# Taking the conditioning's products two rows of blocks at a time

## The chip, the cores and the metric

The kernel runs on one core of a Trainium2 chip. The metric is device time in microseconds (us) of one launch. Engines are named as the profile names them: PE is TensorE's matmul, PEld its weight load, DVE VectorE, ACT ScalarE, POOL GpSimd, SP the engine that issues most of the loads. A "record" is one matmul as the trace shows it; the float32 products of the conditioning have two records each.

## The reference

Two blocks run one after the other over 512 tokens of 1024 channels. The first has two layers with a mixer (an mLSTM, a Fourier mixing and a convolution) and an MLP, over x and 256 further tokens of context; the second has attention and is not touched here. Each layer of the first block is conditioned: two vectors (`c` and `c_ctx`) are multiplied by a matrix of 1024 x 6144 a layer, and the six parts of 1024 shift, scale and gate the norms:

```python
for l in range(DEPTH):
    mx = jnp.split((jax.nn.silu(c) @ w_ada[l] + b_ada[l])[:, None, :], 6, axis=-1)
    mc = jnp.split((jax.nn.silu(c_ctx) @ w_ada[l] + b_ada[l])[None, None, :], 6, axis=-1)
    hx = modulate(rmsnorm(x, g_pre_mix[l]), mx[0], mx[1])
    hc = modulate(rmsnorm(ctx, g_pre_mix[l]), mc[0], mc[1])
    out_x, out_c = token_mixers(hx, hc, ...)
    x = x + mx[2] * rmsnorm(out_x, g_post_mix[l])
    hx = modulate(rmsnorm(x, g_pre_mlp[l]), mx[3], mx[4])
    x = x + mx[5] * rmsnorm(sq_relu_mlp(hx, w_mlp1[l], w_mlp2[l]), g_post_mlp[l])
```

So `w_ada` is 48 MB of weights for two vectors: much to load, little to multiply. Everything is float32.

## The kernel before, in words

The program is written once, in the order of the computation, through a `Recorder`; nothing is issued then. `schedule` orders each engine's instructions by priority and readiness with estimated durations, and gives each buffer its place, kind by kind, from a fixed number (`KINDS`: 3 raw weights `wr`, 2 high parts `wh`, 2 low parts `wl`, 4 and 3 PSUM banks `pm` and `pd`, 1 bank `pa`). Then everything is issued engine by engine in that order, and each engine runs its stream strictly in order, waiting for the others by semaphores. All recorded instructions stand on one line of the source (L358), so rows are told apart by their tiles.

A weight tile (`weight`) is a load of 512 KB into `wr`, a copy to `wh` by ACT (the high part), a subtraction to `wl` by DVE (the low part), and then three products a block on PE: high by high, high by low, low by high. In the MLP of the first block, `strassen` takes two weight tiles at once, forms sums of their quarters (on POOL and DVE, in place in `wr`) and makes seven products of quarters. Names: `wr<-in_w_in` are weights of the mixers, `wr<-in_w_mlp` of the MLP, `wr<-in_w_ada` rows of the conditioning.

The conditioning is cut into 12 units (`l`, `u`: two layers with six parts) of 8 rows of blocks each. `ada_steps` (L528 to 540) makes a list of 8 small functions for a unit. One such step loads a row, 128 x 1024, into a `wr` buffer and multiplies it: four products of 256 columns each (`128*32 128x256`, 32 stationary columns), which go to four sets of 32 rows of one PSUM tile `pa`. After the eighth row `ada_end` copies the sums from PSUM (`ftmp<-pa`, DVE), turns them on PE and adds the biases on DVE.

The steps are run from other code, to lie beside its work:

- the first two units at the start, from buffers of the kind `slot` (rows `pa<-slot,const`);
- 16 steps in the mixers of layer 0: `feed` holds them, and `weight` (L453) and `strassen` (L1301, twice a call) pop one step for each weight tile;
- 24 steps in the mLSTM outputs of layer 0 and 16 in those of layer 1 (list `back`, popped evenly over the chunks, L1172);
- 24 steps in the MLP of layer 0 (`feed.extend(mid)`, L1381), popped as the weight tiles come: 4 in `plain`, then in turn 4 in four weight tiles of `product2` and 2 in each of two calls of `strassen` (`fast`), and so on.

A run of products on `pa` between other work on PE is called a visit below. The program's text:

Of the kernel before, what the change touches and what calls it, by code (L numbers as in the profile page):

```python
# [33 lines left out]
# which engine takes the pairs of a norm's steps: v for Vector, p for Pool, a for Activation  # L34
ADD, MUL, AFF, LO = "vpvp", "vvvv", "avav", "vpvp"
# buffers: how many there are, and how many have to stay free when one is taken out of turn
# [8 lines left out]
class View:  # L45
    """A region of a buffer that gets its place only when the order of the instructions is known."""
# [49 lines left out]
    def bits(self):  # L96
        """the columns as the bits of a number"""
        m = np.zeros(self.buf.cols, np.uint8)
        m[self.idx.reshape(-1)] = 1
        return int.from_bytes(np.packbits(m).tobytes(), "big")  # L100
# [36 lines left out]
class Recorder:  # L137
    """Takes the program as it is written, orders each engine's instructions by priority and readiness with
    estimated durations, places the buffers, and then issues everything in that order."""
# [86 lines left out]
    def schedule(self):  # L226
        """List scheduling. A buffer's kind is served in program order."""
# [32 lines left out]
        def place(o):  # L260
            """places the buffers that the instruction is the first to touch, if they are all to be had"""
# [99 lines left out]
def tile_net(tc: tile.TileContext, A, out):  # L361
# [55 lines left out]
    def csum(srcs, n, w=0):  # L417
        """the mean over the channels of some blocks, on every partition"""
        ps = pm()[:, :n]
        for i, x in enumerate(srcs):  # L420
            pe.matmul(ps, onesD[:, w], x, start=i == 0, stop=i == len(srcs) - 1)
        return ps
# [7 lines left out]
    def add_square(acc, o, sl, n, first):  # L430
        """adds the squares of a block to a tile of sums"""
# [16 lines left out]
    feed = []  # L448
    HP, EP, RP = 3000, 3500, 100

    def weight(src, place=("wh", "wl"), nk=8, by=HP):
# [6 lines left out]
        if feed:  # L458
            feed.pop(0)()
# [23 lines left out]
    def run(blocks, acts, evac, order=R8, nk=None):  # L483
        """blocks: (key, source, groups); one weight tile after the other, all its tokens"""
# [5 lines left out]
    def narrow(src, acts, groups, evac):  # L490
        """a block of 32 columns: its high and low parts side by side, their products in two sets of rows"""
# [15 lines left out]
    def run_outer(blocks, acts, evac, groups, done=None, order=R8, ready=(), before=None):  # L507
        """as run, but group by group over a few resident weight tiles"""
# [19 lines left out]
    def ada_steps(l, u, place="wr"):  # L528
        st = K()

        def step(k):
            if k == 0:
                st.ps = pa()
            raw = rec.buf(place, [P, 1024], F32)
            ld(raw, A["w_ada"][l, u, k])
            for j in range(4):
                pe.matmul(st.ps[32 * j:32 * j + 32, 0:TC], cs[:, k, :], raw[:, j * TC:(j + 1) * TC], start=k == 0, stop=k == 7)
            if k == 7:
                ada_end(l, u, st.ps)
        return [lambda k=k: step(k) for k in range(8)]  # L540
# [23 lines left out]
    def pre(l, kind):  # L564
        """the gain and shift before the mixers (0) or the MLP (2), by conditioning"""
# [9 lines left out]
    def modulate(r, g, hs, gs, rs):  # L575
        """the next input of the matrix products: r * rs * gain + shift, in the two parts, r as four pairs of blocks"""
# [46 lines left out]
    def post_chain(g, o_, qs, old, hs, gs, gain=None):  # L623
        """the residual plus norm(o), kept in o's place and in DRAM, then the next norm"""
# [19 lines left out]
    def pairs():  # L644
        """activations in two parts: four tiles of [part, block of the pair, token]"""
# [26 lines left out]
    def rope_tables():  # L672
        """the cosines and signed sines by position, kept in DRAM until the second block"""
# [64 lines left out]
    def rows_of_three():  # L738
        """rows of the tokens of x, three to a slot"""
# [9 lines left out]
    class Later:  # L749
        """the tokens of x alone, by their place among all"""  # L750
# [7 lines left out]
    def gates(S, GX):  # L758
# [26 lines left out]
        # each head has two rows: the first of them takes the high part, the second the low one  # L785
# [46 lines left out]
    def mixers(l, hs, back, steps):  # L832
# [6 lines left out]
        # Fourier input and half of the conv module's  # L839
# [11 lines left out]
        # Fourier mixing: the sums over pairs of tokens s and n - s feed the cosines, the differences the sines,  # L851
        # and the results for t and n - t share both
# [46 lines left out]
        # conv module input  # L899
# [71 lines left out]
        # keys, values, queries  # L971
# [43 lines left out]
        # output gate  # L1015
# [10 lines left out]
        # mLSTM states before each chunk, both directions  # L1026
# [28 lines left out]
        # mLSTM outputs  # L1055
# [130 lines left out]
    # ---- the MLP's first product: tokens in two halves (A and B), channels in two halves, and the pairs of hidden  # L1186
    # blocks make seven products of quarters instead of eight (Strassen's algorithm as Winograd has it)
    def taker(n):
        """places for pairs of blocks of 256 tokens: first one in each of n slots, then their other two thirds, then more slots"""
# [81 lines left out]
    def strassen(l, src1, src2, parts_of, quarters, b, ev1, tail):  # L1271
# [14 lines left out]
        # the sums S2, S4 take the place of A11, A12 and S3, S1 that of A21, A22 when those have been split  # L1286
# [14 lines left out]
        for _ in range(2):  # L1301
            if feed:
                feed.pop(0)()
# [39 lines left out]
    def layer(l, hs, nxt, steps, back, mid, early=None, norm_mem=None, fill=None):  # L1343
# [7 lines left out]
        # output projection  # L1351
# [28 lines left out]
        # MLP  # L1380
# [189 lines left out]
    def block2(hs):  # L1570
# [8 lines left out]
        # selected and window keys and values, first queries: every block is chosen and the window covers the sequence  # L1579
# [505 lines left out]
```

## Time and profile before

| | us |
|---|---|
| runs | 2058.71, 2059.37, 2061.32 (median 2059.37) |
| span of the profiled execution | 2061.5 |
| PE busy | 1965.2 (95%) |
| PE weight loads busy | 1672.1 |
| DVE busy | 1386.3 |
| ACT busy | 878.3 |
| POOL busy | 501.9 |

The page gives the span of the profiled execution, from its first to its last instruction; it lies 0.1% above the median of the runs and within 0.2 us of the slowest. Busy shares are averages over stages with different limits; for a single stage the timeline and the stretches are read. A line of the timeline merges neighbouring instructions of one form: start, duration from the first's start to the last's end, and xcount. Neighbours on PE overlap, so that what a group costs the stream is the time from its start to the next line's start. Square brackets at a line's end are idle time before it and who ended it.

### The profile page before, as it was taken

How to read it: one execution, taken by the hardware profiler on the slowest of the kernel's cores; microseconds unless marked ns; L12 is line 12 of the kernel's file. 1: busy time of each engine (PE TensorE's matmuls, PEld its weight loads, DVE VectorE, ACT ScalarE, POOL GpSimd, SP SyncE). 2: the span in 40 equal slices, each digit the busy share in tenths (PEclk: the TensorE clock that was granted, in tenths of full speed). 3: DMA queues.
4: the chain of work that ended last, by engine and by line, in shares of the span. 5: the costliest groups of instructions: out<-in, count | busy, mean ns of one | idle time of the engine just before them, and what ended most of it. 6: DMA issues, size and time to landing. Idle time of an engine off the chain costs nothing.

```text
span 2061.5 us, 32412 instructions
## 1 busy us (share of the span) xinstructions
PE 1965.2 (95%) x12772; PEld 1672.1 (81%) x12772; DVE 1386.3 (67%) x2380; ACT 878.3 (43%) x1699; POOL 501.9 (24%) x486
## 2 busy tenths in 40 slices
PE   5999998988999999999899998899999998999999
PEld 3978885877988999999788886788989897776676
DVE  6588677287545665566878775887787785465664
ACT  4433355454322332234543355544343464553442
POOL 2210141245211222113320051542232232111210
PEclk8999998999999999999999999999999999999999
DMA  8233335251433221122321234322323342200201
GB/s 296 89 106 104 122 129 185 76 185 52 132 104 123 72 73 41 62 83 103 118 84 52 72 134 164 103 82 93 113 83 123 117 162 81 83 31 32 79 26 59
DMA packets 82570, 207.47 MB, mean 101 GB/s; under 512 B 8945, under 2 KB 36849, under 8 KB 82418
## 3 DMA queue, kind: packets, MB, share of 16 engines
q1 hardware_dynamic: 66690, 189.13, 27.0%
q10 hardware_dynamic: 15728, 16.27, 2.3%
q8 instruction: 100, 1.64, 0.3%
q14 instruction: 52, 0.43, 0.1%
HBM read 189.12 MB, written 16.25 MB: 100 GB/s over the span
## 4 chain that ended last, share of the span: by engine, by line
PE 65%; DVE 8%; issue 2%; ACT 1%; POOL 1%; DMA 1%; DVEq 0%; POOLq 0%; ACTq 0%
PE pd L358 44%; PE pm L358 18%; DVE slot L358 5%; PE pa L358 4%; DVE tmp L358 2%; DVE wl L358 1%; POOL slot L358 1%; ACT slot L358 0%; DMA wr<-in_w_ada 0%; ACT tmp L358 0%; ACT rs L358 0%; ACT wh L358 0%; DVE small L358 0%; POOL ftmp L358 0%; DMA wr<-in_w_in 0%
## 5 line engine op out<-in xcount | busy, mean ns | idle before, releaser
L358 PE MATMUL pd<-slot,wh 128*128 128x256 f32 (+2 forms) x4384 | 1092.2, 341 | 18.4 <-DVE slot L358 12.4
L358 PEld LDWEIGHTS pd<-slot,wh 128*128 128x128 f32 (+1 forms) x4384 | 745.1, 189 | 127.6 <-issue 18.7
L358 PE MATMUL pd<-slot,wl 128*128 128x256 f32 (+1 forms) x2136 | 724.1, 340 | 5.8 <-DVE wl L358 5.6
L358 PEld LDWEIGHTS pd<-slot,wl 128*128 128x128 f32 x2136 | 406.8, 191 | 55.0 <-DVE wl L358 7.7
L358 ACT ACTIVATE wh<-wr 128x1024 fp32r<-128x1024 f32 (+2 forms) x202 | 205.0, 1015 | 425.0 <-PE pd L358 388.1
L358 DVE TENSOR_TENSOR wl<-wr,wh 128x1024 fp32r<-128x1024 f32 (+2 forms) x199 | 248.4, 1248 | 129.1 <-ACT wh L358 128.2
L358 PE MATMUL pm<-slot,slot 128*128 128x256 f32 (+4 forms) x1674 | 256.7, 297 | 2.1 <-DVE tmp L358 1.6
L358 PEld LDWEIGHTS pm<-slot,slot 128*128 128x128 f32 (+1 forms) x1674 | 216.7, 191 | 28.2 <-issue 14.4
L358 DVE TENSOR_TENSOR slot<-pd,slot 128x512 f32<-128x512 f32 (+1 forms) x208 | 119.4, 574 | 127.0 <-PE pd L358 124.4
L358 PE MATMUL pd<-slot,slot 128*128 128x256 f32 (+1 forms) x1048 | 146.9, 289 | 2.9 <-ACT slot L358 2.6
L358 PEld LDWEIGHTS pd<-slot,slot 128*128 128x128 f32 x1048 | 132.8, 191 | 7.6 <-ACT slot L358 3.8
L358 DVE TENSOR_TENSOR slot<-ftmp,slot 128x512 fp32r<-128x512 f32 (+2 forms) x116 | 93.5, 809 | 36.1 <-POOL ftmp L358 34.5
L358 ACT ACTIVATE tmp<-tmp 128x512 f32<-128x512 f32 (+3 forms) x122 | 62.2, 545 | 126.9 <-DVE tmp L358 125.8
L358 DVE SCALAR_TENSOR_TENSOR slot<-slot,const,slot 128x512 f32<-128x512 f32 (+2 forms) x184 | 113.2, 664 | 0.8
L358 POOL TENSOR_TENSOR ftmp<-tmp 128x512 f32<-128x512 f32 x54 | 58.5, 1104 | 214.5 <-ACT tmp L358 214.5
L358 POOL TENSOR_TENSOR wr<-wr 128x512 f32<-128x512 f32 x27 | 39.3, 1455 | 290.0 <-DVE wl L358 248.9
L358 POOL TENSOR_TENSOR ftmp<-ftmp 128x256 f32<-128x256 f32 (+1 forms) x72 | 66.1, 918 | 166.7 <-ACT ftmp L358 162.5
L358 ACT ACTIVATE slot<-tmp 128x512 fp32r<-128x512 f32 (+1 forms) x134 | 80.7, 628 | 58.8 <-DVE tmp L358 38.8
L358 DVE TENSOR_TENSOR slot<-wr,slot 128x512 fp32r<-128x512 f32 (+1 forms) x85 | 87.3, 1033 | 17.2 <-ACT slot L358 17.2
L358 PE MATMUL pm<-slot,wh 128*128 128x256 f32 x544 | 98.4, 281 | 0.0
L358 ACT ACTIVATE slot<-wr 128x512 fp32r<-128x512 f32 (+1 forms) x85 | 72.0, 855 | 44.7 <-POOL wr L358 22.4
L358 PEld LDWEIGHTS pm<-slot,wh 128*128 128x128 f32 x544 | 84.0, 188 | 2.8 <-issue 1.6
(202 smaller groups left out, 2478.2 us busy)
## 6 DMA issues: line engine op xcount, KB each, us to landing
wr<-in_w_mlp SPq DMA_DIRECT2D x128, 512.0 KB, 3.4
wr<-in_w_ada SPq DMA_DIRECT2D x80, 512.0 KB, 4.0
wr<-in_w_in SPq DMA_DIRECT2D x66, 512.0 KB, 3.3
dram<-slot ACTq DMA_DIRECT2D x52, 256.0 KB, 2.5
tmp<-dram SPq DMA_DIRECT2D x40, 256.0 KB, 3.8
slot<-in_w_ada SPq DMA_DIRECT2D x16, 512.0 KB, 10.1
wr<-in_w_out SPq DMA_DIRECT2D x16, 512.0 KB, 3.9
wr<-in_w_out SPq DMA_DIRECT2D x8, 384.0 KB, 2.9
```

The lines of the kernel that those rows point to most:

```text
L358: o.fn(*[conv(x) for x in o.a], **{k: conv(x) for k, x in o.k.items()})
```

## The change

A step now takes two rows: it takes two raw buffers, issues both loads, and makes the eight products. A unit is a list of four such steps. The first product of a step (`k == k0 and j == 0`) waits also for the second row's load (`after=last`); the other products wait for their own row alone. `feed_one` pops a step only at every second call, so that a pair goes with two weight tiles. The lists `back` become half as long, 12 and 8 functions, and are popped evenly as before. Comments and docstrings are removed too, which moves line numbers.

```diff
-    feed = []
+    feed, turns = [], itertools.count()
     HP, EP, RP = 3000, 3500, 100
+
+    def feed_one():
+        if feed and next(turns) % 2:
+            feed.pop(0)()
...
-        if feed:
-            feed.pop(0)()
+        feed_one()
         return wh, wl
...
-        def step(k):
-            if k == 0:
+        def step(k0):
+            if k0 == 0:
                 st.ps = pa()
-            raw = rec.buf(place, [P, 1024], F32)
-            ld(raw, A["w_ada"][l, u, k])
-            for j in range(4):
-                pe.matmul(st.ps[32 * j:32 * j + 32, 0:TC], cs[:, k, :], raw[:, j * TC:(j + 1) * TC], start=k == 0, stop=k == 7)
-            if k == 7:
+            raws = [rec.buf(place, [P, 1024], F32) for _ in range(2)]
+            for k, raw in enumerate(raws, k0):
+                last = sp.dma_start(out=raw, in_=A["w_ada"][l, u, k])
+            for k, raw in enumerate(raws, k0):
+                for j in range(4):
+                    pe.matmul(st.ps[32 * j:32 * j + 32, 0:TC], cs[:, k, :], raw[:, j * TC:(j + 1) * TC],
+                              start=k == 0, stop=k == 7, after=last if k == k0 and j == 0 else None)
+            if k0 == 6:
                 ada_end(l, u, st.ps)
-        return [lambda k=k: step(k) for k in range(8)]
+        return [lambda k=k: step(k) for k in range(0, 8, 2)]
...
         for _ in range(2):
-            if feed:
-                feed.pop(0)()
+            feed_one()
```

What stands in the order of PE in the mixers of layer 0, before (`wr` is a row of w_ada, `const` the vectors, xN counts products; a second weight tile begins behind the row):

```order
L358 MATMUL pd_185_1171<-slot_81_370,wh_166_1069 128x256
L358 MATMUL pd_185_1171<-slot_83_377,wh_166_1069 128x256
L358 MATMUL pd_185_1171<-slot_81_370,wl_170_1090 128x256
L358 MATMUL pa_173_1108<-wr_172_1104,const_13_91 32x256 x4
L358 MATMUL pd_189_1220<-slot_70_327,wh_174_1111 128x512
L358 MATMUL pd_189_1220<-slot_74_339,wh_174_1111 128x512
L358 MATMUL pd_189_1220<-slot_70_327,wl_177_1126 128x512
```
and now, at the same place:

```order
L358 MATMUL pd_183_1164<-slot_83_376,wh_166_1069 128x256
L358 MATMUL pd_183_1164<-slot_81_369,wl_170_1090 128x256
L358 MATMUL pa_184_1198<-wr_162_1030,const_13_91 32x256 x4
L358 MATMUL pa_184_1198<-wr_172_1104,const_13_91 32x256 x4
L358 MATMUL pd_189_1221<-slot_70_327,wh_174_1111 128x512
L358 MATMUL pd_189_1221<-slot_74_339,wh_174_1111 128x512
L358 MATMUL pd_189_1221<-slot_70_327,wl_175_1121 128x512
```
Two rows of four products stand together; the four that stood at the next weight tile before are gone from there.

The order of PE in the MLP of layer 0, where the first call of `strassen` begins, before:

```order
L358 MATMUL pd_771_5092<-slot_680_4442,wl_754_4972 128x256
L358 MATMUL pd_771_5092<-slot_695_4542,wh_751_4960 128x256 x2
L358 MATMUL pd_771_5092<-slot_695_4542,wl_754_4972 128x256
L358 MATMUL pa_772_5106<-wr_762_5036,const_13_91 32x256 x4
L358 MATMUL pm_774_5113<-slot_611_4061,wh_760_5029 128x256
L358 MATMUL pm_774_5113<-slot_616_4075,wh_760_5029 128x256
```
and now:

```order
L358 MATMUL pd_771_5092<-slot_678_4437,wh_752_4961 128x256 x2
L358 MATMUL pd_771_5092<-slot_678_4437,wl_753_4969 128x256
L358 MATMUL pd_771_5092<-slot_694_4540,wh_752_4961 128x256 x2
L358 MATMUL pd_771_5092<-slot_694_4540,wl_753_4969 128x256
L358 MATMUL pa_772_5106<-wr_763_5039,const_13_91 32x256 x3
L358 MATMUL pm_774_5112<-slot_611_4061,wh_759_5023 128x256
```
The first row's last three products stand where its four stood. The rest of the pair stands some 90 instructions later, inside the run of that call's `pm<-slot,slot`:

```order
L358 MATMUL pm_774_5112<-slot_710_4667,slot_781_5170 128x256 x2
L358 MATMUL pm_774_5112<-slot_710_4667,slot_784_5184 128x256
L358 MATMUL pm_774_5112<-slot_733_4815,slot_781_5170 128x256 x2
L358 MATMUL pm_774_5112<-slot_733_4815,slot_784_5184 128x256
L358 MATMUL pa_772_5106<-wr_763_5039,const_13_91 32x256
L358 MATMUL pa_772_5106<-wr_787_5198,const_13_91 32x256 x4
L358 MATMUL pm_774_5112<-slot_733_4815,slot_781_5170 128x256 x2
```
The first row's first product, the one that waits for both loads, comes with the second row's four. In the order of PE as a whole, the visits to rows in `wr` number 74 before, 46 of them of four products; now 59, of which 15 have eight products, 15 have five and 12 have three.

The order of SP, which issues the loads, around that call, before:

```order
L358 DMA wr_753_4967<-in_w_mlp 128x1024
L358 DMA wr_755_4980<-in_w_mlp 128x1024
L358 DMA wr_762_5036<-in_w_ada 128x1024
L358 DMA wr_775_5116<-in_w_ada 128x1024
L358 DMA wr_783_5177<-in_w_mlp 128x1024
L358 DMA wr_787_5196<-in_w_mlp 128x1024
L358 DMA wr_792_5235<-in_w_ada 128x1024
```
and now:

```order
L358 DMA wr_754_4976<-in_w_mlp 128x1024
L358 DMA wr_760_5029<-in_w_mlp 128x1024
L358 DMA wr_763_5039<-in_w_ada 128x1024
L358 DMA wr_787_5198<-in_w_ada 128x1024
L358 DMA wr_789_5230<-in_w_mlp 128x1024
L358 DMA wr_793_5251<-in_w_mlp 128x1024
L358 DMA wr_794_5258<-in_w_ada 128x1024
```
The two rows come behind two weights. `wr_763` and `wr_787` are the two rows of the pair that PE takes as three and five, and the two weights behind them (`wr_789`, `wr_793`) are those of the call of `strassen` that follows.

## Rows read from the trace of the kernel before

**Rows 1.** The page: the span; busy time of the engines; the chain that ended last by engine.

```profile
span 2061.5 us, 32412 instructions
...
PE 1965.2 (95%) x12772; PEld 1672.1 (81%) x12772; DVE 1386.3 (67%) x2380; ACT 878.3 (43%) x1699; POOL 501.9 (24%) x486
...
PE 65%; DVE 8%; issue 2%; ACT 1%; POOL 1%; DMA 1%; DVEq 0%; POOLq 0%; ACTq 0%
```

**Rows 2.** Who PE waited for, over the whole span: us in total, times, longest.

```profile
PE pm L358 <- DVE tmp L358: 25.0, 21, 4.1
...
PE pm L358 <- DVE ftmp L358: 10.1, 7, 5.7
...
PE pd L358 <- DVE wl L358: 5.6, 3, 3.8
...
PE pa L358 <- DMA wr<-in_w_ada: 1.7, 3, 1.0
```

**Rows 3.** The instructions that write `pa` from rows in `wr`: duration in ns, least, median and most; first and last start.

```profile
L358 PE MATMUL pa<-wr,const x640: 379/379/636, 116.0 to 1251.0; 128*32 128x256 f32 x160
```

**Rows 4.** PE's timeline around a lone row of the conditioning (start, duration, xcount).

```profile
522.65 0.28 PE L358 MATMUL pd<-slot,wl 128*128 128x256 f32 x1
522.76 0.40 PE L358 MATMUL pd<-slot,wh 128*128 128x256 f32 x2
...
523.36 0.28 PE L358 MATMUL pd<-slot,wl 128*128 128x256 f32 x1
523.56 0.64 PE L358 MATMUL pa<-wr,const 128*32 128x256 f32 x8
524.13 0.72 PE L358 MATMUL pd<-slot,wh 128*128 128x512 f32 x2
524.69 0.40 PE L358 MATMUL pd<-slot,wl 128*128 128x512 f32 x1
524.93 0.63 PE L358 MATMUL pd<-slot,wh 128*128 128x512 f32 x2
525.40 0.38 PE L358 MATMUL pm<-const,ftmp 128*128 128x128 f32 x2
```

**Rows 5.** PE's timeline at four visits of other sizes in the mLSTM outputs of layer 0: five, eight, one and three products (two records each), each with the line behind it.

```profile
291.28 1.05 PE L358 MATMUL pa<-wr,const 128*32 128x256 f32 x10
292.26 0.49 PE L358 MATMUL pd<-slot,slot 104*128 104x512 f32 x1
...
329.84 1.07 PE L358 MATMUL pa<-wr,const 128*32 128x256 f32 x16
330.84 0.38 PE L358 MATMUL pd<-slot,slot 128*128 128x128 f32 x1
...
342.79 0.62 PE L358 MATMUL pa<-wr,const 128*32 128x256 f32 x2
343.34 0.49 PE L358 MATMUL pm<-slot,slot 128*128 128x129 f32 x2
...
348.25 0.63 PE L358 MATMUL pa<-wr,const 128*32 128x256 f32 x6
348.81 0.38 PE L358 MATMUL pm<-slot,slot 128*128 128x129 f32 x1
```

**Rows 6.** PE's timeline, the lines with a long wait ahead of them, in the mixers of layer 0 (the gates; the mLSTM outputs) and at the start of its MLP.

```profile
140.70 0.42 PE L358 MATMUL pm<-small,const 36*128 36x48 f32 x2 [2.90 <-DVE small L358]
...
314.58 0.69 PE L358 MATMUL pm<-const,ftmp 128*128 128x128 f32 x2 [5.75 <-DVE ftmp L358]
...
459.64 1.10 PE L358 MATMUL pm<-tmp,const 128*128 128x256 f32 x4 [1.89 <-DVE tmp L358]
...
486.96 0.50 PE L358 MATMUL pd<-slot,wl 128*128 128x512 f32 x1 [0.68 <-DVE wl L358]
493.57 0.58 PE L358 MATMUL pd<-slot,wh 128*128 128x256 f32 x1 [3.55 <-DVE slot L358]
495.24 0.58 PE L358 MATMUL pd<-slot,wh 128*128 128x256 f32 x1 [0.66 <-DVE slot L358]
498.26 0.58 PE L358 MATMUL pd<-slot,wh 128*128 128x256 f32 x1 [2.02 <-DVE slot L358]
```

**Rows 7.** SP's timeline in the mixers of layer 0: when loads were issued.

```profile
126.66 0.33 SPq L358 DMA_DIRECT2D wr<-in_w_in  x1
131.23 0.33 SPq L358 DMA_DIRECT2D wr<-in_w_ada  x1
135.80 0.33 SPq L358 DMA_DIRECT2D wr<-in_w_in  x1
```

**Rows 8.** The page's loads: count, KB each, median us from issue to landing.

```profile
wr<-in_w_mlp SPq DMA_DIRECT2D x128, 512.0 KB, 3.4
wr<-in_w_ada SPq DMA_DIRECT2D x80, 512.0 KB, 4.0
wr<-in_w_in SPq DMA_DIRECT2D x66, 512.0 KB, 3.3
...
wr<-in_w_out SPq DMA_DIRECT2D x16, 512.0 KB, 3.9
```

**Rows 9.** Who SP's queue waited for, over the whole span: us in total, times, longest.

```profile
SPq L358 <- DVE wl L358: 687.7, 108, 30.2
...
SPq L358 <- PE pa L358: 313.4, 65, 13.3
```

**Rows 10.** SP's timeline in the MLP of layer 0, behind two calls of `strassen`.

```profile
553.62 0.33 SPq L358 DMA_DIRECT2D wr<-in_w_mlp  x1
556.02 0.33 SPq L358 DMA_DIRECT2D wr<-in_w_ada  x1
```

**Rows 11.** PE's timeline at the end of the second of these calls.

```profile
567.18 0.64 PE L358 MATMUL pa<-wr,const 128*32 128x256 f32 x8
567.75 0.73 PE L358 MATMUL pd<-slot,wh 128*128 128x512 f32 x2
```

**Rows 12.** The page's costliest groups: the copy to the high part and the subtraction to the low part (busy, mean ns of one, idle before them).

```profile
L358 ACT ACTIVATE wh<-wr 128x1024 fp32r<-128x1024 f32 (+2 forms) x202 | 205.0, 1015 | 425.0 <-PE pd L358 388.1
L358 DVE TENSOR_TENSOR wl<-wr,wh 128x1024 fp32r<-128x1024 f32 (+2 forms) x199 | 248.4, 1248 | 129.1 <-ACT wh L358 128.2
```

**Rows 13.** Busy time of each engine in a stretch of the span (start:end and length; PE, PEld, DVE, ACT, POOL with counts; granted clock of PE as a share of full speed, share of the DMA engines, GB/s).

```profile
1200.00:1260.00 60.00, 53.81 (x427) 39.52 (x426) 45.18 (x149) 31.43 (x88) 16.59 (x16) 0.94 0.53 185
```

## The prediction

> **What bounds the kernel now.** I read the page first [rows 1]: TensorE (PE) is busy 95% of 2061.5 us and makes 65% of the chain that ended last; the next engine on that chain, VectorE (DVE), makes 8%. So the change is worth what it takes from PE's own time, plus or minus the few waits in which PE stands still. The list of PE's waits [rows 2] says who ends them: nearly all end with DVE, and the conditioning's rows from HBM have kept PE waiting 1.7 us in three places. A missing row of w_ada is therefore not what the kernel loses time to, and a change of the conditioning acts through the PE time of its products, through the order of the work around them, and through the ring of three weight buffers (`wr`) that its rows share with the weight tiles.
>
> The products themselves: 640 records for 320 matmuls, two of each, 379 ns at the median [rows 3]. Their price in the stream is not that duration, as neighbours overlap; it is read from start to start in PE's timeline. A lone row of blocks (4 matmuls, 8 records) begins at 523.56 and the next product at 524.13: 0.57 us [rows 4]. Around it the stream loses more: 523.36 to 523.56 is 0.20 us where the same kind of product takes 0.11 (522.65 to 522.76), and the two after it take 0.56 from 524.13 to 524.69 where the same two take 0.47 with nothing ahead (from 524.93 to 525.40). So a visit costs 0.09 + 0.09 = 0.18 us for coming and going, and 0.57 for its work: 0.75.
>
> Where two rows already come together (16 records) the work takes 1.00 us, 329.84 to 330.84 [rows 5]: with the same 0.18, 1.18 for a pair, against 1.50 for two lone rows. **Each merged pair is worth 0.32 us.** The other rows of that group tell what a pair in pieces costs: 1 matmul 0.55, 3 matmuls 0.56, 5 matmuls 0.98 us. The price goes up by fours (one for each of the four column groups, which run beside each other), so a pair cut into 3 and 5 costs 0.56 + 0.98 + 2 x 0.18 = 1.90 us, **0.40 more than two lone rows**.
>
> The Trainium skill (TensorEngine Tiling (Array Packing), Key Properties) says that changing the tiling mode, not just the tile, drains TensorE. The 0.18 us around a visit agree in kind. By that rule alone only the number of visits would count (74 before, 59 after); the rows show that how many matmuls stand in a visit counts as well, and that decides the MLP below.
>
> **The change part by part.** The matmuls (320 in all) and the loads into `wr` (80) stay as many; in the order of the changed kernel PE makes 59 visits to them instead of 74. By place:
>
> A. Layer 0's keys, values, queries and output gate (116 to 271 us): 16 lone visits become 8 whole pairs. 8 x 0.32 = 2.6 us less PE work. Part goes to a wait: at 140.70 PE waits 2.90 us for the gates' chain on DVE [rows 6]. Three visits stood ahead of that, one pair does now: 3 x 0.75 - 1.18 = 1.1 us earlier there, and the chain ends no sooner, so 1.1 us becomes wait. Net -1.5 us; both ends: -2.6 (nothing absorbed) and -0.5 (another wait absorbs as much). The loads cover it: now weight tile and row alternate 4.6 us apart (126.66, 131.23, 135.80, [rows 7]); two weights and then two rows need the same 4 loads per 18 us at 3.3 to 4.0 us each [rows 8].
>
> B. Layer 0's mLSTM outputs (291 to 355 us): 21 visits become 19, but some pairs are cut in 3 and 5. Three merges of 0.32 against two or three cuts of 0.40: nothing, to a tenth. The last pair now needs both rows in place before its first product, which delays the end of the stage and the output projection's first loads by about a microsecond at most (one load's 3.9 us, less what the ring already makes it wait). PE's wait of 5.75 us at 314.58 is DVE's and its instructions there keep their order. 0, from -0.5 to +1.
>
> C. Layer 0's MLP (442 to 666 us). The first matmul of a pair waits for the second row's load, the other three of the first row do not, and the planner places them when the first row is in. So in the new order seven of eleven pairs stand as 3 and 5, and only four whole. Before: 22 lone visits (the first two rows together aside, which stay as they are). PE work: 7 x 0.40 - 4 x 0.32 = **+1.5 us**. In a Strassen call the five stand inside a run of 24 matmuls of `pm<-slot,slot`, so until then the first row keeps one of the three buffers, and with the second row two of them. SP's queue waits for such buffers already: 313 us in 65 waits for PE's `pa` matmuls, 688 for DVE's split [rows 9]. What is late next: the weight that was asked for at 553.62 and whose products start behind the step of 567.18 [rows 10, 11]. It has 567.75 - 553.62 = 14.1 us; it needs 3.4 to land [rows 8], 1.0 on ScalarE and 1.2 on DVE [rows 12], some 5.6 in all. Placed behind the five and behind the split's own chain, I estimate its start at 561 to 562, which leaves about 6 us: at the edge. This is twice per stage (each second Strassen call). Bounds: nothing, or 2 us each time; I take 0.4 each, near the lower end because the cover is still just above the need: +0.8. DVE's order around 450 to 500 us also changes (the norm's chain against the split of weights), where PE waits 1.89, 0.68, 3.55, 0.66 and 2.02 us for DVE [rows 6], 8.8 in all. No row prices an order that hasn't run; a reordering may give or take a fourth of that, I guess: 0, from -2 to +2. C: 1.5 + 0.8 = +2.3, from 1.5 - 2 = -0.5 to 1.5 + 4 + 2 = +7.5.
>
> D. Layer 1's mLSTM outputs (1210 to 1251 us): 13 visits become 12, with one or two cuts. PE is busy 53.8 of 60 us there [rows 13], the densest DMA of all stretches (0.53). 0, from -0.7 to +0.7.
>
> At the start the rows of the first two units already stand side by side and have their own buffers: nothing. From 1260 us on both kernels issue the same instructions in the same order: nothing.
>
> Sum: -1.5 + 0 + 2.3 + 0 = **+0.8 us**. Made on the profiled execution's span (2061.5 us; its own time lies among 2058.71 to 2061.32, which differ by 0.1% among themselves) and put on the median of 2059.37: **2060.2 us**. 0.2%, 4.1 us, is what a measurement of this kernel can tell from no change; the forecast is no change.
>
> **The rivals.**
> 1. Only visits count (the mode change is the price and cuts cost nothing more). Then 15 fewer visits at 0.18 + 0.14 = 0.32 us: -4.8, less 1.1 in the wait at 140.70: -3.7 us, 2055.7. For it: each visit has its own coming and going. Against it: 1 matmul took 0.55 us and 5 took 0.98, which is no linear price. It passes 0.2% only if the wait absorbs nothing (-4.8, 2054.6) or DVE's waits in C shrink too. Chance of a time below 2055.2 in this way or through DVE's new order at 450 to 500: 0.14.
> 2. The ring starves (the slower side). One mechanism: in C a pair holds two of three `wr` buffers until its five products, and each weight behind it starts late. It decides from the point where a weight's start slips more than 14.1 - 5.6 = 8.5 us. Four Strassen calls and seven cut pairs: at 1 to 2 us for each Strassen call +4 to +8, in place of the 0.8 above: 2063.5 to 2067.5. For it: SP already spends 313 us waiting for `pa`. Against it: today PE lost only 1.7 us to w_ada and 5.6 to DVE's `wl` over the whole kernel. Chance of more than +4.1 us in this way or through that same order of DVE: 0.20.
> 3. The change doesn't do what it says: pairs stay whole in A alone, and elsewhere the planner cuts most of them. That is the forecast itself (A gains, C pays). The opposite, all of C's pairs whole, would make C 11 x -0.32 + 0.8 = -2.7 and the sum -4.2: 2055.2. PE takes its instructions in the order written and some 90 others stand between the three and the five, so it has a chance of 0.02, inside "no change".
>
> **How the numbers follow.** Forecast with its own range, 2057 to 2063.5 (the stalls at 0 to 2 us each, or DVE's order by its 2 us): 0.55; rivals 1 and 3 short of 0.2%: 0.11; so no change 0.66, faster 0.14 (rival 1), slower 0.20 (rival 2). The range to hold the time 8 times in 10 reaches down to rival 1 with nothing absorbed, 2054.6, and up to A's -1.5 with C's +7.5 and half of B's bound, +6.5: 2065.9. It leaves out less than a tenth on either side.
>
> **What would show it.** Right: 8 groups of 16 records of `pa<-wr,const` between 116 and 271 us, each 1.00 us to the next product, and PE's wait at the gates grown from 2.9 towards 4.0; groups of 6 and 10 records in the MLP at 0.56 and 0.98 us; PE's busy time within 2 us of before. Wrong: a wait of PE for `wl` or `wh` near 550 to 570 and 620 to 640 above 1 us (rival 2), waits at 450 to 500 that differ from 8.8 us by more than 2, or pairs that stand in one group in the MLP. If the stretch from 442 to 666 us gets shorter, the price of the cuts was wrong.

## The result, and the profile after

The changed kernel takes 2071.24 us (median of four runs, 2069.11 to 2071.42), the kernel before, beside it, 2060.35 (2058.71 to 2062.38): the ratio is 1.0064, with a 95% interval from 1.0047 to 1.0080. It is **slower by some 11 us**, 0.5 to 0.8%. The forecast was 2060.2 us and no change, with 0.20 for slower and 2065.9 as the upper end of the range: wrong. The profiled execution of the changed kernel is its fastest, 2069.11 us with a span of 2067.3; the span before was 2061.5. In all other runs the span is 1.7 to 1.9 us less than the time, so the traced execution of the kernel before took some 2063.3 us, longer than any of its four runs here (and 2 us more than the slowest of the first three): the two traces therefore show 5.8 of the 11 us. Of the 24 runs of the kernel before that stand beside the first four experiments, one took 5253.63 us at a granted clock of 0.361; it is counted in their median of 2059.63, which is 2059.48 without it.

The page of the changed kernel, its span, busy times, and the chain that ended last by engine (beside [rows 1]):

```profile
span 2067.3 us, 32409 instructions
...
PE 1963.6 (95%) x12772; PEld 1676.0 (81%) x12772; DVE 1388.9 (67%) x2380; ACT 878.7 (43%) x1699; POOL 505.9 (24%) x486
...
PE 64%; DVE 9%; ACT 2%; issue 2%; POOL 1%; DMA 1%; DVEq 0%; ACTq 0%; POOLq 0%
```

PE is busy 1.6 us less and the span is 5.8 us longer: the loss is not in PE's busy time but in its waits, and the chain says where to look, since DVE and ACT have a percent more each.

PE takes the same number of instructions in both, and outside the stages that the change touches it takes them in the same order. So the start of the same instruction in both traces tells where time is won or lost. The changed kernel is ahead of the old one by 1.7 us at 109 us of the old trace (by chance of the execution: nothing there is touched but the first loads), by 4.5 at 270 (4.0 at 272, when both have their 16 rows there behind them), by 2.8 at 288, by 1.8 at 388 and at 455, by 2.4 at 488; it is **behind by 1.1 us at 499** and by 5.8 at 679; from there to 993 the difference stays at 5.8 to 5.9. Between 993 and 1400 it moves between 7.8 and 4.0 and settles at 5.1, mostly at places where both take the same instructions in the same order; at the end it is again 5.8. In short: mixers -2.3, then +1.2 and +1.1 back; MLP of layer 0 **+7.6**.

**The products cost what was forecast.** PE's timeline at the first pair, and at the two halves of a cut pair in the MLP (beside [rows 4, 5]):

```profile
123.27 0.28 PE L358 MATMUL pd<-slot,wl 128*128 128x256 f32 x1
123.48 1.07 PE L358 MATMUL pa<-wr,const 128*32 128x256 f32 x16
124.48 0.73 PE L358 MATMUL pd<-slot,wh 128*128 128x512 f32 x2
...
534.27 0.63 PE L358 MATMUL pa<-wr,const 128*32 128x256 f32 x6
534.83 0.50 PE L358 MATMUL pm<-slot,wh 128*128 128x256 f32 x2
...
546.12 1.05 PE L358 MATMUL pa<-wr,const 128*32 128x256 f32 x10
547.10 0.74 PE L358 MATMUL pm<-slot,slot 128*128 128x256 f32 x4
```

A whole pair takes 1.00 us to the next product, three products 0.56 and five 0.98, as read before. Three of PE's waits take part of the mixers' gain (the first beside [rows 6]):

```profile
138.69 0.42 PE L358 MATMUL pm<-small,const 36*128 36x48 f32 x2 [3.23 <-DVE small L358]
...
269.19 0.33 PE L358 MATMUL pm<-const,ftmp 128*128 128x128 f32 x1 [0.27 <-DVE ftmp L358]
272.24 1.13 PE L358 MATMUL pm<-tmp,slot 128*128 128x129 f32 x8 [0.58 <-DVE const L358]
```

The wait at the gates grew by 0.33 us (2.90 to 3.23), and the two later ones, which are new, belong to the 1.2 us that are given back between 272 and 288 us.

**The first jump in the MLP, 3.5 us, is in three waits.** PE's timeline of the changed kernel, its waits between 484 and 500 us (beside the last four of [rows 6]):

```profile
484.57 0.50 PE L358 MATMUL pd<-slot,wl 128*128 128x512 f32 x1 [1.06 <-DVE wl L358]
487.64 0.39 PE L358 MATMUL pd<-slot,wh 128*128 128x256 f32 x1 [0.38 <-DVE slot L358]
491.19 0.58 PE L358 MATMUL pd<-slot,wh 128*128 128x256 f32 x1 [2.94 <-DVE slot L358]
494.23 0.58 PE L358 MATMUL pd<-slot,wh 128*128 128x256 f32 x1 [2.03 <-DVE slot L358]
495.80 0.58 PE L358 MATMUL pd<-slot,wh 128*128 128x256 f32 x1 [0.78 <-ACT slot L358]
499.33 0.58 PE L358 MATMUL pd<-slot,wh 128*128 128x256 f32 x1 [2.95 <-DVE slot L358]
```

Before, these waits sum to 6.9 us; now they sum to 10.1. At the same instructions of PE, the wait of 2.03 us was 0.66 before (495.24 in [rows 6]), the one of 0.78, for ACT, is new, and the last, 2.95, was 2.02 (498.26). From start to start the three cost 1.4, 1.0 and 1.1 us. What DVE does meanwhile, in the kernel before:

```profile
493.11 0.41 DVE L358 TENSOR_TENSOR slot<-ftmp,slot 128x256 fp32r<-128x256 f32 x1
...
494.76 0.42 DVE L358 TENSOR_TENSOR slot<-ftmp,slot 128x256 fp32r<-128x256 f32 x1
...
495.70 1.10 DVE L358 TENSOR_TENSOR slot<-tmp,slot 128x512 fp32r<-128x512 f32 x1
496.72 1.48 DVE L358 TENSOR_TENSOR slot<-ftmp,slot 128x256 fp32r<-128x256 f32 x1
498.13 2.96 DVE L358 TENSOR_TENSOR slot<-tmp,slot 128x512 fp32r<-128x512 f32 x3
```

and in the changed kernel:

```profile
489.66 1.48 DVE L358 TENSOR_TENSOR slot<-ftmp,slot 128x256 fp32r<-128x256 f32 x1
491.06 1.76 DVE L358 TENSOR_TENSOR slot<-tmp,slot 128x512 fp32r<-128x512 f32 x1
...
493.76 0.41 DVE L358 TENSOR_TENSOR slot<-ftmp,slot 128x256 fp32r<-128x256 f32 x1
...
495.47 3.47 DVE L358 TENSOR_TENSOR slot<-tmp,slot 128x512 fp32r<-128x512 f32 x3 [0.70 <-ACT slot L358]
498.87 0.41 DVE L358 TENSOR_TENSOR slot<-ftmp,slot 128x256 fp32r<-128x256 f32 x1
501.10 0.69 DVE L358 TENSOR_TENSOR slot<-tmp,slot 128x512 fp32r<-128x512 f32 x1 [1.82 <-ACT slot L358]
```

The short `slot<-ftmp` are low parts of the first hidden blocks, for which PE waits; the long `slot<-tmp,slot` are low parts of sums that `strassen` needs some 35 us later. Before, one long one stood between the third last and the last of the short ones, and three came after. Now four stand between them, three of these right ahead of the last, and PE resumes at 499.33, when that one has run. The change doesn't touch either; the planner ordered DVE anew because other instructions came at other estimated times.

**The rest of the MLP, 4.7 us, is cut pairs and a late weight** (0.6 of it by 509 us, where PE's granted clock is lower for longer after the waits: 0.50 from 502 to 504 us and 0.78 from 504 to 506, where it was 0.61 and 1.00 before). From 509 to 679 us of the old trace there were 18 lone visits; now three pairs are whole and six are cut. The weight that the prediction looked at (asked for at 553.62 before, [rows 10]) is asked for at 564.61. From the timeline of all engines, first the kernel before, ACT's copy and DVE's subtraction for it, then the changed one, SP's load, the copy, the subtraction, and PE:

```profile
557.25 1.06 ACT L358 ACTIVATE wh<-wr 128x1024 fp32r<-128x1024 f32 x1 [1.12 <-PE pd L358]
...
558.34 1.23 DVE L358 TENSOR_TENSOR wl<-wr,wh 128x1024 fp32r<-128x1024 f32 x1 [0.64 <-ACT wh L358]
```

```profile
564.61 1.71 SPq L358 DMA_DIRECT2D wr<-in_w_mlp  x2
...
567.75 1.06 ACT L358 ACTIVATE wh<-wr 128x1024 fp32r<-128x1024 f32 x1 [3.71 <-DMA wr<-in_w_mlp]
...
570.24 1.22 DVE L358 TENSOR_TENSOR wl<-wr,wh 128x1024 fp32r<-128x1024 f32 x1
...
571.51 0.50 PE L358 MATMUL pd<-slot,wl 128*128 128x512 f32 x1 [0.40 <-DVE wl L358]
```

The load begins 11 us later (10 beside PE, which is 1 us behind by then), ACT waits 3.71 us for it, and the low part is ready at 571.46 where it had been at 559.57. PE comes to it 0.40 us too early. The same happens at 644.99.

### The profile page after: what moved, and what is told of

The parts are those of the page before. It is cut to its first block, busy times and chain, and to the rows that moved or that the text cites. A ratio compares the mean times of both kernels' runs of the same rounds, so it can differ in the third digit from the quotient of the medians.

```text
span 2067.3 us, 32409 instructions
## 1 busy us (share of the span) xinstructions
PE 1963.6 (95%) x12772; PEld 1676.0 (81%) x12772; DVE 1388.9 (67%) x2380; ACT 878.7 (43%) x1699; POOL 505.9 (24%) x486
## 4 chain that ended last, share of the span: by engine, by line
PE 64%; DVE 9%; ACT 2%; issue 2%; POOL 1%; DMA 1%; DVEq 0%; ACTq 0%; POOLq 0%
PE pd L358 43%; PE pm L358 18%; DVE slot L358 5%; PE pa L358 4%; DVE tmp L358 3%; ACT slot L358 1%; DVE wl L358 1%; POOL tmp L358 0%; POOL slot L358 0%; POOL ftmp L358 0%; ACT tmp L358 0%; ACT wh L358 0%; DVE small L358 0%; ACT rs L358 0%; DMA wr<-in_w_mlp 0%
```

## The experiments

One source holds all of them. `MODE` says for each unit how its steps are made: `p` the pairs of the changed kernel, `w` pairs whose first row waits whole, `s` single rows as before (with every weight tile), `d` two single rows with every second weight tile, without the wait for the second row's load. (The three runs that mix kinds within the MLP tell by a mark on each step whether it goes with every weight tile; the code below is that of the others.)

```diff
+        def one(k):
...
+        def two(k0):
+            one(k0)
+            one(k0 + 1)
...
-                              start=k == 0, stop=k == 7, after=last if k == k0 and j == 0 else None)
+                              start=k == 0, stop=k == 7, after=last if k == k0 and (j == 0 or mode == "w") else None)
...
-        if feed and next(turns) % 2:
+        if feed and (every[0] or next(turns) % 2):
```

The theory after the two traces: the loss sits in the MLP of layer 0, half of it in DVE's order at 490 to 500 us, half in the cut pairs and what they hold up. The rivals: it sits in the mLSTM outputs; it is the ring of buffers alone; it is the pairs' loads, however the products stand. All times below are medians of 5 to 12 runs, against the kernel before on the same chip (23 to 31 runs); the ratios, with 95% intervals, are not made from these medians and can differ from them a little.

**Pairs in the mixers alone** (units `p` there, all else `s`).

> Pairs with every second weight tile in layer 0's mixers alone (16 steps, 8 whole pairs); all other steps as before, one row at a time. Theory M (the loss sits in layer 0's MLP): the 8 merged pairs pay, -1.5 to -2.8 us against the kernel before. Rival B (the loss sits in the mLSTM outputs and before them, whose loads meet those of the pairs): what A gains is lost by 290 us, 0 to +2 us. The full change measured +10.9 us on medians.

Measured: 2057.72 us against 2059.63, -1.9 us; ratio 0.9995 (0.9985 to 1.0005). As the theory has it, though the interval holds no change too. In its trace it gains 2.3 us on the old one between 109 and 272 us and gives 1.2 back by 288, just as the changed kernel does.

**Pairs in the MLP alone**.

> Pairs in the MLP of layer 0 alone (24 steps, cut as in the changed kernel); all else as before. Theory M: +6 to +9 us against the kernel before, with PE's waits for DVE at 485 to 500 us 3 us longer, stalls of 2 us in all at the first weight tile behind each pair of strassen calls, and 1.6 us for cut pairs. Rival B: +2 us or less, the cuts alone.

Measured: 2067.85 us against 2059.63, **+8.2 us**; ratio 1.0041 (1.0026 to 1.0056). Three quarters of the loss is here, and the waits stand at the same places, 2.96 us at 499.02, and for `wl` at 570.73 and 643.93.

**Pairs everywhere but in the MLP**.

> The changed kernel, with the MLP's 24 steps one row at a time with every weight tile as before; pairs everywhere else. Theory M: the loss is gone, -1 to +2 us against the kernel before. Rival B: +5 us or more stay.

Measured: 2061.38 us against 2059.63, +1.75 us; ratio 1.0011 (0.9999 to 1.0023). With the run before it, the MLP is settled as the place of most of the loss. It also says that something outside it costs what the mixers gain (3.7 us more than the mixers alone).

**Whole pairs everywhere** (`w`).

> The changed kernel, but all four products of a pair's first row wait for the second row's load, so that every pair stands whole in the order (11 pairs of 8 in the MLP, no 3 and 5). Theory cut (cut pairs and the buffers they hold make the loss): the seven cuts go, -5 us of PE work against the changed kernel, and the stalls behind the strassen calls go too: +3 to +5 us against the kernel before, or less. Rival order (the loss is that every second weight tile and two rows at a time change when the loads and DVE's split come, however the products stand): +9 us or more against the kernel before.

Measured: 2076.01 us against 2059.63, +16.4 us; ratio 1.0076 (1.0058 to 1.0093). The theory of the cuts misses by 11 us, and the rival's number holds, but not for its reason: no pair in the MLP is cut any more, and the MLP (444 to 679 us of the old trace) costs 6.2 us in place of 7.6, little of the 5 that the arithmetic of the visits gave, as PE waits more. **The new loss** is in the mLSTM outputs of layer 0, where this kernel loses 5.8 us against the old one between 288 and 388 us. PE's timeline of this run, three of its waits there:

```profile
306.73 0.47 PE L358 MATMUL pd<-slot,slot 104*128 104x512 f32 x1 [3.60 <-DVE slot L358]
...
333.28 0.64 PE L358 MATMUL pa<-wr,const 128*32 128x256 f32 x8 [1.27 <-DMA wr<-in_w_ada]
...
356.92 0.64 PE L358 MATMUL pa<-wr,const 128*32 128x256 f32 x8 [1.70 <-DMA wr<-in_w_ada]
```

PE itself stands for the second row, 1.27 and 1.70 us: 3.0 of the 5.8. (The 3.60 us stand where 0.30 stood before, but the wait of 5.75 at 314.58 falls to 1.21: together they are 1.2 us less.) The rest is not traced to a cause here. A pair that waits to be whole puts its wait on the engine that is busy 95% of the span.

**Halving the MLP's loss.** First pairs in the first unit of the MLP's steps alone, then in the other two alone.

> Pairs in the MLP of layer 0 for its first 8 steps alone (one unit: one cut pair, then three whole; its first weights and the first second product), the other 16 one row at a time as before. Theory order (half of the MLP's loss is a wait at 485 to 500 us: DVE is given three long subtractions of the sums for the next stage ahead of the last short one that PE waits for): +2.5 to +4.5 us against the kernel before, all of it between 480 and 510 us. Rival ring (the loss is buffers held by pairs in strassen calls): within 1 us of the kernel before.

> The complement: in the MLP of layer 0 the first 8 steps one row at a time as before, the other 16 in pairs (6 cut, 2 whole). Theory order: +3.5 to +4.5 us against the kernel before (cuts 6 x 0.4 - 2 x 0.3 = 1.8 us, and some 2 us of stalls at the first weight tiles behind the strassen calls), nothing at 480 to 510 us. Rival ring: all of the +8 us that pairs in the MLP cost.

Measured: +3.5 us (2063.09 against 2059.55; ratio 1.0022, 1.0012 to 1.0032) and +4.0 us (2063.59; 1.0024, 1.0012 to 1.0036). The two halves add up to 7.6, near the 8.2 of all. In the trace of the first, 3.5 us are lost between the instructions at 488 and 499 us of the old trace, with the same last wait:

```profile
500.31 0.58 PE L358 MATMUL pd<-slot,wh 128*128 128x256 f32 x1 [2.95 <-DVE slot L358]
```

In the trace of the second, nothing is lost there; it loses 3.6 us from 499 to 679. The rival, the ring alone, expected the first at zero and the second at 8: it falls.

**DVE's short instruction put ahead by one dependency.** The long ones of the second half now have to come after the last short one.

```diff
-                    split(hi, lo, t)
+                    A_(hi, t, AF.Copy)
+                    vec.tensor_tensor(lo, t, hi.bitcast(F32), op=ALU.subtract, after=low[0] if p and not l else None)
...
-            vec.tensor_tensor(al, t2, ah.bitcast(F32), op=ALU.subtract)
+            low[0] = vec.tensor_tensor(al, t2, ah.bitcast(F32), op=ALU.subtract)
```

> As the run with pairs in the MLP alone (+8.2 us), with one more dependency on DVE itself: the low parts of the second half of the sums come after the last low part of the first hidden blocks, which is the order that DVE had before. Nothing else is asked for. Theory order: PE's wait of 2.96 us there goes, 3 us of the 8 come back, +4 to +6 us against the kernel before. Rival: PE waits as long for ACT or for another instruction, no more than 1 us comes back.

Measured: 2062.77 us against 2059.55, **+3.2 us** in place of +8.2; ratio 1.0021 (1.0010 to 1.0031). DVE's timeline in this run, then PE's:

```profile
491.53 0.55 DVE L358 TENSOR_TENSOR slot<-ftmp,slot 128x256 fp32r<-128x256 f32 x1 [1.07 <-ACT slot L358]
492.00 2.37 DVE L358 TENSOR_TENSOR slot<-tmp,slot 128x512 fp32r<-128x512 f32 x2
```

```profile
491.48 1.24 PE L358 MATMUL pd<-slot,wh 128*128 128x256 f32 x2 [0.77 <-ACT slot L358]
492.51 0.41 PE L358 MATMUL pd<-slot,wl 128*128 128x256 f32 x1
```

DVE waits 1.07 us and takes the short one first, and PE, after the 0.77 that it waits without the dependency too, goes on with hardly a gap. Waiting for the right instruction is cheaper here than working on the wrong one. Between the instructions at 488 and 499 us of the old trace this run loses 0.6 us, not 3.5. It is not quite the old order, as the expectation has it: before, one long instruction (495.70) ran ahead of the short one and PE's last wait was 2.02 us, while now none does and that wait is gone; the waits of 2.03 and 0.77 stay. Whether the kernel before would gain by the same dependency was not tried. The same dependency in the changed kernel as a whole:

> The changed kernel whole, with DVE's order at 490 to 500 us put back by the one dependency of the run with DVE's order (low parts of the second half of the sums after the last low part of the first hidden blocks). Theory order: +5 to +8 us against the kernel before instead of +10.9. Rival: the wait comes back elsewhere, +9 us or more.

Measured: 2065.44 us against 2058.99, +6.5 us; ratio 1.0035 (1.0023 to 1.0047): 4.4 us of the 10.9 come back. In the traces both runs get back 2.9 us between the instructions at 488 and 499 us. That long instructions of DVE ahead of the short one cost PE these 2.9 us is shown; where the medians (5.0 and 4.4) have more is not.

**Two single rows with every second weight tile, in the MLP alone** (`d`).

> In the MLP of layer 0 two single steps with every second weight tile, without the wait for the second row: each row's four products stand when its own load is in (six merges of eleven by chance, no cut). Theory cut (cuts and the wait for the second row are the loss): -2 us of PE work against the kernel before, and the time about that. Theory order (the loads by twos upset the order of DVE and the ring, however the products stand): +3 us or more.

Measured: 2060.93 us against 2059.55, +1.4 us; ratio 1.0004 (0.9996 to 1.0013). Between the two: DVE's order is the wrong one here too (PE's last wait, 2.96 us, ends at 501.67), but nothing is cut, PE has no wait at all from 560 to 575 us, and it gains 1.6 us from 499 to 679 where the pairs lose 4. So what the second half of the loss needs is the cut, or the rows held for it, and not loads that come by twos.

**Where the rest lies: the mLSTM outputs.**

> Pairs in the mLSTM outputs alone (24 steps in layer 0, 16 in layer 1), all else as before. By the two runs before this should be what separates the run without the MLP (+1.75) from the run with the mixers alone (-1.9): +2 to +4 us against the kernel before. Forecast of the prediction for the two places together: 0, from -1.2 to +1.7.

Measured: +3.8 us (2062.75 against 2058.99; ratio 1.0021, 1.0009 to 1.0033). Its trace, however, loses 0.15 us from 288 to 388 us and nothing at 1200 to 1290. So the two places were tried apart.

> Pairs in the mLSTM outputs of layer 0 alone (24 steps). The two places together measured +3.8 us on medians, while the trace of that run shows only +0.15 us from 260 to 390 us and nothing at 1200 to 1290. If its cost lies in this place: +2 to +4 us against the kernel before, and the stretch from 290 to 390 us longer by as much. If it doesn't: within 1 us.

> Pairs in the mLSTM outputs of layer 1 alone (16 steps). If the cost lies here: +2 to +4 us, the stretch from 1200 to 1290 us longer by as much. If neither of the two shows more than 1 us, the +3.8 was the granted clock in other stretches, which differs by 1.4 to 1.6 us a place between executions of the same instructions.

Measured: +3.1 us (2061.48 against 2058.34; ratio 1.0017, 1.0007 to 1.0027) and +2.6 us (2060.95; 1.0012, 1.0001 to 1.0023). Both intervals lie just above no change, and both profiled executions were among the fastest of their kernels, at 2055.9 and 2056.7 us: against the kernel before, the first gains 0.1 us from 285 to 386 us, where its pairs are, and the second gains 1.1 from 1200 to 1290. So the stretches with the pairs are not longer in these traces. For that case the last expectation names the granted clock in other stretches, and the runs' clocks speak for it in part: their mean is 0.9787 and 0.9784, where 23 runs of the kernel before have 0.9801, and among these 23 a run with 0.001 less was 1.2 us longer on average; by that, an estimate from these runs, 1.7 of the 3.1 us and 2.1 of the 2.6 go with a lower clock (in the run with both places 0.9782 against 0.9794, by the 29 runs beside it 1.3 of the 3.8). **This part stays open**: pairs in the outputs cost some 3 us on medians, no trace shows where, and why the clock was lower is not shown. The two alone add up to 5.7 us and not to 3.8, which the intervals allow.

**Two versions that use what was learned.**

> Pairs in layer 0's mixers, two single steps with every second weight tile in its MLP together with DVE's order of before, the outputs as before. Sum of the single runs: -1.9 (mixers), +1.4 (two singles), -3.5 to -5 (DVE's order): -4 to -5.5 us against the kernel before. Rival (the gains don't add, since a wait for DVE absorbs what comes early): -1.9 or less of a gain.

> Pairs in layer 0's mixers, the MLP's first 8 steps as before, its other 16 as two single steps with every second weight tile, the outputs as before. -1.9 and -1.4 of PE work (the four merges of 0.33 that stand in this order): -3 us against the kernel before. Rival: as above, -1.9 or less of a gain.

Measured: -1.6 us (2057.38 against 2058.99; ratio 0.9989, 0.9980 to 0.9999) and **-2.65 us** (2056.34; 0.9986, 0.9977 to 0.9995). The second is the fastest kernel here: pairs in the mixers, the MLP's first unit as it was, and the others by twos without the wait. It beats the kernel before by about what was expected (-3), and so the changed one. The first gave less than half of the -4 to -5.5 that the single runs add up to; the rival's number (-1.9 or less of a gain) holds, and its reason was not traced.

## Why the prediction was wrong

**The bound and the price of a visit: right.** PE's busy time fell by 1.6 us, within the 2 us named. Whole pairs took 1.00 us, threes 0.56 and fives 0.98 to the next product, as [rows 5] had them. The rival by which only visits count falls: with 15 visits fewer the kernel is slower, and the cuts cost what the four column groups say. The rule of the Trainium skill that stood beside it (TensorEngine Tiling (Array Packing), Key Properties), that a change of the tiling mode drains TensorE, agrees in kind with the 0.18 us around each visit; it does not give the time of a cut.

**A: right in sum, wrong in its place.** 2.7 us less PE work was measured, for 2.6 forecast: 2.3 in the trace at 272 us, and the 0.33 by which the wait at the gates grew. That wait was to grow by 1.1; but PE came to it only 0.6 us earlier, and DVE's chain ended 0.3 earlier (138.69, for 140.70 before, with 1.7 us ahead from the start). And 1.2 us went later, at 272 to 288 us, which no step had named. Net -1.1 in the trace (-1.9 on medians, no clear gain), for -1.5 forecast.

**C is the step that failed: +2.3 us forecast, +7.6 in the trace, +8.2 alone.** By its terms:
- the cuts, 7 x 0.40 - 4 x 0.32 = +1.5: as forecast. By the measured visits, 7 x (0.76 + 1.18) + 4 x 1.20 against 22 x 0.76 is +1.7;
- the stalls behind the strassen calls, +0.8 forecast. Named at the right places (the weight of 553.62, twice in the stage), mis-sized: its load slipped by 10 to 11 us, not by the 8 that were estimated. PE's new waits from 570 to 645 us are 0.15 + 0.40 and 0.19 + 0.15 + 0.40, 1.3 us as recorded; from start to start they cost 2.1, as the products beside a wait follow less closely;
- DVE's order at 450 to 500 us, "0, from -2 to +2": measured +3.5 in the trace, 2.5 of it in two waits for DVE and 1.0 in one for ACT, and one dependency on DVE gave 2.9 back there (5.0 on medians with pairs in the MLP alone, 4.4 with the whole change). **This is the term that broke the forecast.** The places and the engine were named, and the sign of being wrong that went with them came: the waits at 450 to 500 us sum to 11.3 and not to 8.8. That nothing could be said of the sign of the term was taken for a zero with small bounds. The order of DVE could have been read as those of PE and SP were: four `slot<-tmp,slot` between the third last and the last `slot<-ftmp` where one stood, and PE's last wait of 2.02 us ([rows 6]) ends with that last one. Three of them took 2.96 us in a row in the trace of before. Three more ahead of what PE waits for are a price of some 3 us that could be worked out before any run.

**B and D, 0 forecast**: +1.1 (288 to 388 us) and -0.7 (1200 to 1290) in the traces, at the edge of the bounds, and the run with the mixers alone, without pairs in B, has +0.7 in B's place too; +3.8 us together on medians, which is outside, and explained in part at most. The traces' 5.8 us would lie inside the range, the medians' 10.9 do not: the traced execution of the kernel before was 3 us above its median, that of the changed kernel 2 us below.

**Rival 2** came nearest in size (2063.5 to 2067.5) and had half of the mechanism: weights behind a cut pair do come late. But by itself, 2.1 us in the trace, it is the smaller part; its chance of 0.20 covered DVE's order too. **Rival 3's** opposite, whole pairs in C, was priced at -2.7 there and measured +6.2, in the run with whole pairs everywhere, which was 5.5 us worse than the change. The price counted PE's work and not the waits that come with it: for DVE in C, and for the second row in the outputs.

The sum of the parts measured alone, -1.9 + 8.2 + 3.8 = 10.1 us, is close to the 10.9 of the whole; each part has an interval of 2 to 3 us on either side.

## What to carry to other kernels

When a planner writes the order, a small change anywhere orders other engines anew, and that can cost more than the change: go through the engine that the bound engine waits for, find the instruction that ends each of its waits, and look at what the new order puts ahead of it: here three more instructions of 2.96 us in a row cost 3.5 us. Here a group that could begin when its first input was in, and couldn't end without its second, was cut and held buffers in between; independent steps side by side gave six of the eleven merges without either. And where the engine that is busy 95% had to wait for two loads to be both in, it stood 1.3 and 1.7 us.

## What the runs showed of the hardware

The same kernel's time spreads by up to 10 us (2053.09 to 2062.91 in 23 runs of the kernel before), more than most of these effects, and the granted clock is one reason: over these 23 runs it lies between 0.976 and 0.985, and a run with 0.001 less was 1.2 us longer on average (correlation -0.90). Two runs, that with the mixers alone and that without the MLP, have the same instructions in the same order at 1800 to 1860 us, and PE is busy all of it in both. Busy time of the engines in this stretch, and behind POOL's the granted clock, first with the mixers alone, then without the MLP:

```profile
1800.00:1860.00 60.00, 60.00 (x333) 42.89 (x331) 38.82 (x87) 35.45 (x81) 8.11 (x6) 1.00 0.08 27
```

```profile
1800.00:1860.00 60.00, 60.00 (x314) 42.19 (x312) 38.48 (x88) 32.79 (x77) 8.11 (x6) 0.97 0.08 27
```

PE's timeline at one place of it, in the same order:

```profile
1821.93 0.70 PE L358 MATMUL pd<-slot,wh 128*128 128x512 f32 x2
1822.47 0.40 PE L358 MATMUL pd<-slot,wl 128*128 128x512 f32 x1
...
1824.35 0.38 PE L358 MATMUL pm<-const,slot 128*128 128x128 f32 x2
```

```profile
1825.13 0.91 PE L358 MATMUL pd<-slot,wh 128*128 128x512 f32 x2
1825.84 0.63 PE L358 MATMUL pd<-slot,wl 128*128 128x512 f32 x1
...
1829.10 0.38 PE L358 MATMUL pm<-const,slot 128*128 128x128 f32 x2
```

From the first of these lines to the last it is 2.42 us in one and 3.97 in the other: for these products the clock was at its lower level, 1.2 GHz (granted 0.50 from 1826 to 1828 us), and back at 2.4 after (1.00 from 1829). That is 1.55 us in one place, without a wait ahead of it and behind the same products in both. Places of 1.4 to 1.6 us like this differ between executions also around 420 us (granted 0.95 against 1.00 from 395 to 430) and around 1980 (0.97 against 1.00 from 1940 to 2000). A profile of one execution can't settle an effect of this size; it took medians of many runs, and for the mLSTM outputs even these gave no cause.
